# A share of the weight subtractions from VectorE to GpSimd, and all groups of modulation sums on VectorE, in a two-layer gMLP, attention and mixture-of-experts kernel

## The chip, the cores and the metric

The kernel runs on one core of one Trainium2 chip. The metric is the device time of one execution in microseconds; a run gives the median of several executions. The profile comes from one execution with the hardware profiler on, and its times are counted from the start of its span.

The engines of a core are TensorE (PE in the rows; PEld is its loading of weights), VectorE (DVE), ScalarE (ACT), GpSimd (POOL) and SyncE (SP), whose queue issues nearly all loads here. SBUF is the memory of the core that all engines read, PSUM the one in which TensorE leaves its results.

## What is computed

Two layers over 256 tokens of width 1024 (batch 1). Each layer modulates its input by shifts, scales and gates, which come from a conditioning vector `c` of 1024 through large matrices; the first layer mixes tokens with a gMLP, the second with an attention, and both end in a mixture of 64 experts with 8 of them chosen for each token, beside one shared expert.

```
def ada(c, w, b, n):
    m = jax.nn.silu(c) @ w + b
    return [t[:, None, :] for t in jnp.split(m, n, axis=-1)]

def gmlp_mixer(h, w_in, b_in, ln_g, ln_b, w_s, b_s, w_out):
    z = jax.nn.gelu(h @ w_in + b_in)
    u, v = jnp.split(z, 2, axis=-1)
    v = layernorm(v, ln_g, ln_b)
    ...
    sv = jnp.einsum('gts,bcsgd->bctgd', w, v) + b_s.T[None, None, :, :, None]
    return (u * sv.reshape(B, S, A_WIDTH)) @ w_out

def reference(x, c, ...):
    for i in range(DEPTH):                       # 2
        sh1, sc1, g1, sh2, sc2, g2 = ada(c, ada_w[i], ada_b[i], 6)
        h = modulate(rmsnorm(x, norm_mix[i]), sh1, sc1)
        if i < N_A_LAYERS:                       # layer 0
            y = gmlp_mixer(h, ...)
        else:                                    # layer 1
            if kv is None:
                kv = shared_kv(x, c, kv_norm, kv_ada_w, kv_ada_b, kv_w_k, kv_w_v)
            y = moba_mixer(h, ...)
        x = x + g1 * y
        h = modulate(rmsnorm(x, norm_ffn[i]), sh2, sc2)
        x = x + g2 * moe(h, ...)
    return rmsnorm(x, final_norm)
```

## The kernel before

The program is one core's, and its instructions stand on each engine in the order in which they are written (or recorded) below; an engine doesn't pass over one that waits. The stages are the gMLP phase of layer 0, its residual and the routing to experts, the loop over experts, the attention phase of layer 1, residual and routing again, and the second loop over experts.

**Steps and pieces.** The gMLP phase is a list of 48 steps: 16 of the token side (`Tok`, k = 0 to 15), 16 of the feature side (`Feat`, 16 to 31) and 16 of the output (`Out`, 32 to 47). Steps 6 to 47 run in the loop `for k in range(k, n + 16)`. A step multiplies with a 128x1024 part of a weight matrix. For accuracy the part is split in two: ScalarE copies it into the rounded type (`high`, an ACT `scr<-w`), and VectorE subtracts that copy from the original (`low`, a DVE `scr<-w,scr`); TensorE then needs both for three products (`mm3`). `split(steps, k, pool)` issues, in step k, the copy for step k + 3 and the subtraction for step k + 2. Four `scr` tiles are in turn. The attention phase (32 steps) does the same.

**Epilogues.** A `Tok` step ends in an addition on VectorE (`b<-acc`), an `Out` step in VectorE's `h<-wk` and the products after it; `b`, `s`, `h` are tiles of SBUF, `wk` and `acc` are results in PSUM. `BATCH_NORM_STATS2` gathers the layer norm's statistics from `b`.

**Groups of sums.** `ada` is done in groups of four loads of 1 MB: `("a", 2)` to `("a", 5)` for layer 0 (items 8 to 23), `("k", 0)` and `("k", 1)` for the keys and values (items 0 to 7), `("A", 0)` to `("A", 5)` for layer 1. A group listed in `VECTOR` is summed by VectorE: with each load come two instructions of 128x1024 that multiply a part of the load by one element of `silu(c)` and add it (`weigh`; the group's first one is a plain multiplication, `w<-w,cs`). The others are summed by TensorE in `strips`, sixteen matmuls in four takes, and closed by a matmul with `half`. `BEGIN` says in which step a load's sums may be begun, and `tick` lets out of each engine's list as many as the budget of the step (`BUDGET`) allows. In the kernel before, a5, k1 and A5 are summed by TensorE; k1's four takes stand in the routing of layer 0, behind the products `slot` of the routing.

**Loads.** All weights come through 14 slots of 1 MB, in the order of `QUEUE` on SP: one of `ITEMS` alternates with one of `MAIN` (the gMLP's matrices), and the three loads of the shared expert (`("s", 0)`, `wsh`) stand ahead of the last four of `wkva`. Behind them come the loads of experts whose number is known beforehand, and then those that wait for `order`, the list that the routing writes.

**The end of the phase.** `settle` and `close` let out what is left of the sums, `residual` adds the gated result to `xt`; then VectorE and TensorE work out in turns which expert takes which tokens, up to the cast to `order`. TensorE goes on with the gathering of tokens and the shared expert.

Of the kernel before, what the change touches and what calls it, by code (L numbers as in the profile page):

```python
# [33 lines left out]
PRE = 3  # L34
# [4 lines left out]
MAIN = [("i", i) for i in range(PRE, 16)] + [("o", i) for i in range(8)]  # L39
QUEUE = MAIN[:1] + [x for p in zip(ITEMS, MAIN[1:]) for x in p]  # L40
QUEUE += [("s", 0)] + ITEMS[len(MAIN) - 1:]

BEGIN = [(2 * PRE + 2 * i, x) for i, x in enumerate(ITEMS) if 2 * PRE + 2 * i < 46]
BUDGET = ((1.25, 0.9, 0.9), (1.25, 0.9, 0.9), (1.0, 0.9, 0.9))

# [11 lines left out]

VECTOR = [("a", 2), ("a", 3), ("k", 0), ("a", 4)] + [("A", i) for i in range(5)]

# [126 lines left out]
def tile_model(ctx: ExitStack, tc: tile.TileContext, A: dict, out: bass.AP):  # L186
# [86 lines left out]
    def low(t, src, eng=None):  # L273
        (eng or V).tensor_tensor(t[:, 1], src, t[:, 0], ALU.subtract)
# [267 lines left out]

    def split(steps, k, pool):

        if k + LA < len(steps):
            f = steps[k + LA]
            f.h = high(f.part(), pool)
        if 0 <= k + LA - 1 < len(steps):
            f = steps[k + LA - 1]
            low(f.h, f.part())  # L550

# [22 lines left out]
    def tick(tv, ts, tp):  # L574


        for f in list(active):
            if f.done():
                f.age = getattr(f, "age", 0) + 1
                if f.age > 1:  # L580
                    f.finish()
                    active.remove(f)
        for e, t in ((S, ts), (V, tv), (T, tp)):
            credit[e] = min(credit[e], 0) + t
            for f in active:
                while credit[e] > 0 and f.ops[e] and not (e is S and f.left(T)):
                    t, op = f.ops[e].pop(0)
                    op()
                    credit[e] -= t
# [610 lines left out]
    with phase("pb") as pool:  # L1200
# [170 lines left out]
        steps = []  # L1371
# [60 lines left out]
        for k in range(k, n + 16):  # L1432
# [3 lines left out]
            if k in (6, 10):  # L1436
                fetch_bv(512 * (k + 2) // 4, 512)
            split(steps, k, pool)
            e = k + 4 - n
# [20 lines left out]
            if k >= 42:  # L1460
                next(weighing, None)
            tick(*((0, 0.9, 0.9) if k > 45 else BUDGET[k // 16]))
        settle()
# [21 lines left out]
    with phase("pe") as pool:  # L1485
# [158 lines left out]
        for k in range(n):  # L1644
# [4 lines left out]
            if 0 <= j - 1 < 8:  # L1649
                pairs[j - 1].maxima()  # L1650
            split(steps, k, pool)
            if k:
# [18 lines left out]
            for c in range(2 * k - 24, 2 * k - 22) if 12 <= k < 16 else ():  # L1671
# [3 lines left out]
                G.tensor_tensor(hq[1][:, c, :], t, hq[0][:, c, :], ALU.subtract)  # L1675
            tick(*BUDGET1[k // 4])
            if k == WEIGH1 - 1:
# [93 lines left out]
```

## Time and profile before

| | us |
|---|---|
| median of three runs (lowest, highest) | 1399.44 (1397.13, 1403.96) |
| the profiled execution | 1401.17 |
| its span | 1399.4 |
| gMLP phase of layer 0 | 0 to 202 |
| residual, routing up to `order` | 202 to 221 |
| routing's rest, shared expert | 221 to 245 |
| loop over experts, layer 0 (from its start-up on) | 245 to 720 |
| attention phase of layer 1 | 720 to 872 |
| residual and routing, layer 1 | 872 to 960 |
| loop over experts, layer 1 | 960 to 1374 |

The stages are cut from the trace's timeline at instructions that can be named, such as the last matmul of a phase. Over the span PE is busy for 1339.6 us, DVE for 758.0, ACT for 452.2 and POOL for 57.6. The rows that follow are of three kinds: a window row gives the busy time of each engine in a stretch, with the granted clock of TensorE as a share of full speed; a group row puts like instructions of one engine together, with their count, their sum and the mean of one; a timeline row is one instruction (or some like ones in line) with its start and its duration, and in brackets the time that its engine stood idle before it.

### The profile page before, as it was taken

The page shows a single profiled execution, that of the slowest core. Times are in us where ns is not written, and L with a number is a line of the kernel's source. Part 1 is how long each engine was busy: PE and PEld are TensorE (multiplying, and loading weights), DVE is VectorE, ACT ScalarE, POOL GpSimd, SP SyncE. Part 2 cuts the span into 40 slices and gives each one's busy share as a digit, 9 for nine tenths or more (in the row PEclk, how much of TensorE's full clock was granted, in tenths as well). Part 3 has the DMA queues.
Part 4 walks back from the last instruction along what each step waited for, and adds up shares of the span by engine and source line. Part 5 has one row for each costly group of instructions (what it writes and reads, how often), then busy time and mean ns, then how long its engine had stood idle before and what let it go on. Part 6 is the DMA issues. An engine that isn't in the chain of part 4 may idle for free. (4 is left out here: it accounts for less than half of the span.)

```text
span 1399.4 us, 26932 instructions
## 1 busy us (share of the span) xinstructions
PE 1339.6 (96%) x10954; PEld 886.3 (63%) x10954; DVE 758.0 (54%) x1408; ACT 452.2 (32%) x921; POOL 57.6 (4%) x70
## 2 busy tenths in 40 slices
PE   8999999899999999998989999999999999999997
PEld 6899776555655555564649886765565556555553
DVE  3599945444455444444458866554444444444444
ACT  4444424122232222222344543322223222232222
POOL 1000002000000000000010320200000000000000
PEclk8899999999999999999999989999999999999999
DMA  9999876699999999999998855669999999999995
GB/s 387 332 342 360 313 267 240 262 402 425 426 426 425 426 373 426 426 426 426 426 408 318 295 205 216 271 230 394 418 426 426 426 426 425 426 426 426 426 426 218
DMA packets 91128, 516.60 MB, mean 369 GB/s; under 512 B 8308, under 2 KB 8436, under 8 KB 34934
## 3 DMA queue, kind: packets, MB, share of 16 engines
q1 hardware_dynamic: 90420, 513.77, 90.5%
q8 instruction: 88, 1.44, 0.4%
q10 hardware_dynamic: 580, 1.06, 0.2%
q14 instruction: 40, 0.33, 0.1%
HBM read 513.75 MB, written 1.05 MB: 368 GB/s over the span
## 5 line engine op out<-in xcount | busy, mean ns | idle before, releaser
L200 PE MATMUL wk<-w,b 128*32 128x256 f32 (+1 forms) x4928 | 415.6, 387 | 20.2 <-DMA w<-in_wexp_dram 20.2
L200 PEld LDWEIGHTS wk<-w,b 128*32 128x32 f32 (+1 forms) x4928 | 236.0, 123 | 166.2 <-DMA w<-in_wexp_dram 22.4
L200 DVE TENSOR_TENSOR s<-s,s 64x512 fp32r<-64x512 f32 x220 | 151.1, 687 | 123.5 <-ACT s L200 121.8
L200 PE MATMUL wk<-w,ht 128*32 128x512 f32 (+1 forms) x1232 | 211.5, 599 | 0.0
L200 ACT ACTIVATE b<-wk,adaT,sc 128x256 f32<-128x256 f32 x112 | 63.3, 565 | 285.6 <-DVE b L200 285.6
L200 DVE TENSOR_SCALAR b<-wk,sc,adaT 128x256 f32<-128x256 f32 x112 | 60.9, 544 | 156.0 <-PE wk L200 155.8
L200 PE MATMUL wk<-s,b 128*128 128x256 f32 (+2 forms) x1024 | 140.8, 287 | 0.0
L200 ACT CAST s<-s 64x512 fp32r<-64x512 f32 x220 | 134.3, 611 | 15.5 <-DVE s L200 12.8
L200 PEld LDWEIGHTS wk<-s,b 128*128 128x128 f32 (+1 forms) x1024 | 130.9, 187 | 10.3 <-issue 1.1
L200 PE MATMUL acc<-s,h 128*128 128x512 f32 x440 | 132.7, 423 | 0.4 <-DVEq L1147 0.4
L200 DVE TENSOR_TENSOR s<-wk,g 128x512 f32<-128x512 f32 x110 | 76.1, 692 | 89.2 <-PE wk L200 88.9
L200 PEld LDWEIGHTS wk<-w,ht 128*32 128x32 f32 (+1 forms) x1232 | 53.3, 121 | 99.7 <-issue 91.6
L200 ACT ACTIVATE h<-wk 64x256 f32<-64x256 f32 (+1 forms) x114 | 42.9, 376 | 211.7 <-PE wk L200 211.6
L200 DVE SCALAR_TENSOR_TENSOR h<-wk,ws,h 64x256 f32<-64x256 f32 x110 | 54.0, 491 | 98.1 <-ACT h L200 97.3
L200 DVE TENSOR_TENSOR scr<-w,scr 128x1024 fp32r<-128x1024 f32 x80 | 97.5, 1232 | 10.2 <-ACT scr L200 10.1
L200 ACT CAST scr<-w 128x1024 fp32r<-128x1024 f32 x80 | 83.1, 1047 | 51.7 <-PE wk L200 33.2
L200 PEld LDWEIGHTS acc<-s,h 128*128 128x128 f32 x440 | 74.4, 189 | 24.0 <-DVEq L1147 1.1
L200 ACT COPY ht<-wk 128x128 f32<-128x128 f32 x110 | 29.3, 266 | 185.4 <-PE wk L200 185.4
L200 PEld LDWEIGHTS wk<-ident,h 64*128 64x128 f32 (+1 forms) x226 | 22.5, 137 | 94.8 <-DVE h L200 93.9
L200 PE MATMUL wk<-hh,scr 128*128 128x256 f32 x576 | 73.0, 286 | 1.3 <-POOL hh L200 1.3
L200 PEld LDWEIGHTS wk<-hh,scr 128*128 128x128 f32 x576 | 70.5, 194 | 1.7 <-POOL hh L200 1.7
L200 PE MATMUL acc<-scr,hh 128*128 128x256 f32 x384 | 52.9, 299 | 4.8 <-DVE hh L200 4.5
(245 smaller groups left out, 1238.8 us busy)
## 6 DMA issues: line engine op xcount, KB each, us to landing
w<-in_wexp_dram SPq DMA_DIRECT2D x384, 1024.0 KB, 16.6
w<-in_wada_dram SPq DMA_DIRECT2D x48, 1024.0 KB, 7.6
w<-in_win_dram SPq DMA_DIRECT2D x16, 1024.0 KB, 7.5
w<-in_wqkvo_dram SPq DMA_DIRECT2D x16, 1024.0 KB, 7.8
w<-in_wkva_dram SPq DMA_DIRECT2D x8, 1024.0 KB, 6.8
w<-in_wout_dram SPq DMA_DIRECT2D x8, 1024.0 KB, 7.5
w<-in_wsh_dram SPq DMA_DIRECT2D x6, 1024.0 KB, 6.6
xt<-in_x_dram SPq DMA_DIRECT2D x1, 1024.0 KB, 6.4
```

Source lines behind the costliest of these rows:

```text
L200: r = f(*a, **k)
```

## The change

`split` takes an engine: in the odd steps that `HELP` lists, the subtraction goes to GpSimd instead of VectorE, twenty in the gMLP phase's loop (steps 7 to 47, the piece of step 9 on) and six in the attention phase (steps 1 to 11). `VECTOR` now has all groups, so a5, k1 and A5 join VectorE's sums and their strips are gone. The loads of `ITEMS` come at a pace of 1.75 steps instead of 2 and all ahead of the shared expert's. The budgets of VectorE's sums are lower, with 1.1 (0.6 in the attention phase) more in the steps in which GpSimd helps, and the last steps keep a budget. k1 is begun in the gMLP phase.

```
--- before.py
+++ after.py
@@ -37,11 +37,17 @@
 ITEMS = [("a", i) for i in range(8, 16)] + [("k", i) for i in range(4)]
 ITEMS += [("a", i) for i in range(16, 24)] + [("k", i) for i in range(4, 8)]
 MAIN = [("i", i) for i in range(PRE, 16)] + [("o", i) for i in range(8)]
-QUEUE = MAIN[:1] + [x for p in zip(ITEMS, MAIN[1:]) for x in p]
-QUEUE += [("s", 0)] + ITEMS[len(MAIN) - 1:]
-
-BEGIN = [(2 * PRE + 2 * i, x) for i, x in enumerate(ITEMS) if 2 * PRE + 2 * i < 46]
-BUDGET = ((1.25, 0.9, 0.9), (1.25, 0.9, 0.9), (1.0, 0.9, 0.9))
+
+PACE = 1.75
+QUEUE = sorted([(2 * i, x) for i, x in enumerate(MAIN)] + [(1 + PACE * i, x) for i, x in enumerate(ITEMS)],
+               key=lambda x: x[0])
+QUEUE = [x for _, x in QUEUE] + [("s", 0)]
+
+BEGIN = [(2 * PRE + int(PACE * i), x) for i, x in enumerate(ITEMS)]
+BUDGET = ((1.0, 0.9, 0.9), (1.0, 0.9, 0.9), (0.9, 0.9, 0.9))
+
+MORE = 1.1
+HELP = (range(7, 48, 2), range(1, 12, 2))
 
 
 AMONG = [(2, 0)]
@@ -55,7 +61,7 @@
 QUEUE1 = [x for _, x in QUEUE1] + [("s", 0)]
 BUDGET1 = ((1.8, 0.9, 0.9),) * 8
 
-VECTOR = [("a", 2), ("a", 3), ("k", 0), ("a", 4)] + [("A", i) for i in range(5)]
+VECTOR = [("a", i) for i in range(2, 6)] + [("k", i) for i in range(2)] + [("A", i) for i in range(6)]
 
 
 
@@ -540,14 +546,14 @@
                 for tt in range(2):
                     self.ep_(tt, self.p[tt])
 
-    def split(steps, k, pool):
+    def split(steps, k, pool, eng=None):
 
         if k + LA < len(steps):
             f = steps[k + LA]
             f.h = high(f.part(), pool)
         if 0 <= k + LA - 1 < len(steps):
             f = steps[k + LA - 1]
-            low(f.h, f.part())
+            low(f.h, f.part(), eng)
 
     sums = {}
     active = []
@@ -1435,7 +1441,7 @@
                     begin(x)
             if k in (6, 10):
                 fetch_bv(512 * (k + 2) // 4, 512)
-            split(steps, k, pool)
+            split(steps, k, pool, G if k in HELP[0] else V)
             e = k + 4 - n
             if k == n:
                 acc = accs()
@@ -1459,7 +1465,8 @@
                 flush(lambda f: f.dstT is adaT[0] and f.dst is None)
             if k >= 42:
                 next(weighing, None)
-            tick(*((0, 0.9, 0.9) if k > 45 else BUDGET[k // 16]))
+            tv, ts, tp = BUDGET[k // 16]
+            tick(tv + (MORE if k in HELP[0] else 0), ts, tp)
         settle()
         close()
         residual(xt, acc, g1[0])
@@ -1648,7 +1655,7 @@
             j = k - 17
             if 0 <= j - 1 < 8:
                 pairs[j - 1].maxima()
-            split(steps, k, pool)
+            split(steps, k, pool, G if k in HELP[1] else V)
             if k:
                 steps[k - 1].ep()
             if 0 <= j - 1 < 8:
@@ -1673,7 +1680,8 @@
                 S.activation(t, xT[c], AF.Identity, bias=adaT[1][:, c:c + 1], scale=scm[:, c:c + 1])
                 V.tensor_copy(hq[0][:, c, :], t)
                 G.tensor_tensor(hq[1][:, c, :], t, hq[0][:, c, :], ALU.subtract)
-            tick(*BUDGET1[k // 4])
+            tv, ts, tp = BUDGET1[k // 4]
+            tick(tv + (0.6 if k in HELP[1] else 0), ts, tp)
             if k == WEIGH1 - 1:
                 flush(lambda f: f.dst is None)
             if k >= WEIGH1:
```

Three places show how the instructions of the engines stand. The first is VectorE and GpSimd in the middle of the `Tok` steps. VectorE before:

```order
L200 TENSOR_TENSOR scr_848<-w_267,scr_848 128x1024
L200 TENSOR_TENSOR b_91_349<-acc_816,s_131_683 128x256
L200 TENSOR_TENSOR b_92_350<-acc_817,s_131_683 128x256
L200 SCALAR_TENSOR_TENSOR w_265<-w_265,cs,w_261 128x4x256
L200 SCALAR_TENSOR_TENSOR w_265<-w_265,cs 128x4x256
L200 TENSOR_TENSOR scr_875<-w_267,scr_875 128x1024
L200 BN_STATS bn_351<-b_91_349 128x6
L200 BN_STATS bn_352<-b_92_350 128x6
L200 TENSOR_TENSOR scr_910<-w_271,scr_910 128x1024
```

VectorE now:

```order
L206 SCALAR_TENSOR_TENSOR w_265<-w_265,cs,w_261 128x4x256
L206 SCALAR_TENSOR_TENSOR w_265<-w_265,cs 128x4x256
L206 TENSOR_TENSOR scr_848<-w_267,scr_848 128x1024
L206 TENSOR_TENSOR b_91_349<-acc_818,s_131_683 128x256
L206 TENSOR_TENSOR b_92_350<-acc_819,s_131_683 128x256
L206 BN_STATS bn_351<-b_91_349 128x6
L206 BN_STATS bn_352<-b_92_350 128x6
L206 TENSOR_TENSOR adaT_104<-wk_939,pk 128x8
L206 TENSOR_SCALAR w_269<-w_269,cs 128x4x256
L206 SCALAR_TENSOR_TENSOR w_269<-w_269,cs 128x4x256
L206 TENSOR_TENSOR scr_910<-w_273,scr_910 128x1024
```

GpSimd now, where before the `t_27` step was followed by the two of the routing (`t_162`, `t_165`):

```order
L206 TENSOR_TENSOR t_27_176<-t_23_163,mhalf 128x2
L206 TENSOR_TENSOR scr_685<-w_250,scr_685 128x1024
L206 TENSOR_TENSOR scr_749<-w_259,scr_749 128x1024
L206 TENSOR_TENSOR scr_815<-w_263,scr_815 128x1024
L206 TENSOR_TENSOR scr_877<-w_267,scr_877 128x1024
L206 TENSOR_TENSOR scr_951<-w_273,scr_951 128x1024
L206 TENSOR_TENSOR scr_1013<-w_277,scr_1013 128x1024
```

Of two subtractions that stood around the sums, one is now in GpSimd's queue, `scr_877` for example; the sums of VectorE stand one load further on beside the same epilogues.

The second is VectorE at the end of the gMLP phase, ahead of the residual, which begins with `s<-acc,g`. Before:

```order
L200 TENSOR_TENSOR s_256_1854<-b_90_348,s_256_1854 128x256
L200 TENSOR_TENSOR s_43_255<-s_43_255,sc_0_1857 128x512
L200 TENSOR_TENSOR scr_1876<-w_331,scr_1876 128x1024
L200 TENSOR_TENSOR s_263_1897<-b_90_348,s_263_1897 128x256
L200 TENSOR_TENSOR scr_1905<-w_331,scr_1905 128x1024
L200 TENSOR_TENSOR g_102_401<-wk_1963,g_102_401 128x512
L200 TENSOR_TENSOR g_102_401<-wk_1966,g_102_401 128x512
L200 TENSOR_TENSOR s_269_1969<-acc_1570,g_17_143 128x512
```

Now:

```order
L206 TENSOR_TENSOR s_43_255<-s_43_255,sc_0_1864 128x512
L206 SCALAR_TENSOR_TENSOR w_331<-w_331,cs 128x4x256
L206 TENSOR_TENSOR scr_1880<-w_337,scr_1880 128x1024
L206 TENSOR_TENSOR s_264_1901<-b_90_348,s_264_1901 128x256
L206 SCALAR_TENSOR_TENSOR w_335<-w_335,cs,w_331 128x4x256
L206 SCALAR_TENSOR_TENSOR w_335<-w_335,cs 128x4x256
L206 SCALAR_TENSOR_TENSOR w_339<-w_339,cs,w_335 128x4x256
L206 SCALAR_TENSOR_TENSOR w_339<-w_339,cs 128x4x256
L206 TENSOR_TENSOR kvT<-wk_1967,pk 128x8
L206 TENSOR_TENSOR s_269_1977<-acc_1574,g_17_143 128x512
```

The last subtraction of this end is GpSimd's; the last four weighted sums, k1's, and the addition that closes k1 (`kvT`) stand directly ahead of the residual, where the additions to the gate `g` stood.

The third is TensorE in the routing, from the products with `slot` on. Before:

```order
L200 LDWEIGHTS slot_2167
L200 MATMUL wk_2184<-identb,slot_2167 64x128
L200 MATMUL wk_2187<-w_339,cs 32x512 x4
L200 MATMUL wk_2187<-w_341,cs 32x512 x4
L200 MATMUL wk_2187<-w_343,cs 32x512 x4
L200 MATMUL wk_2187<-w_345,cs 32x512 x4
L200 MATMUL wk_2115<-b_299_2080,w_335 128x256 x4
L200 MATMUL wk_2115<-b_299_2080,w_333 128x256 x4
L200 MATMUL wk_2115<-b_299_2080,w_335 128x256 x4
```

Now:

```order
L206 LDWEIGHTS slot_2175
L206 MATMUL wk_2192<-identb,slot_2175 64x128
L206 MATMUL wk_2123<-b_299_2088,w_343 128x256 x4
L206 MATMUL wk_2123<-b_299_2088,w_341 128x256 x4
L206 MATMUL wk_2123<-b_299_2088,w_343 128x256 x4
L206 LDWEIGHTS slotT_2207
L206 MATMUL wk_2225<-pub_2211,slotT_2207 128x112
```

The four takes of `strips` between `slot` and the shared expert's `b,w` are gone, and the shared expert's parts lie in other slots, as its loads are issued later.

## Rows read from the trace of the kernel before

**Rows 1.** Windows: busy us and instructions by engine, granted clock, DMA share, GB/s.

```profile
core 0: us, PE busy (x) PEld busy (x) DVE busy (x) ACT busy (x) POOL busy (x), PEclk, DMA share, GB/s
62.00:138.00 76.00, 76.00 (x663) 75.81 (x661) 73.42 (x88) 39.48 (x59) 1.88 (x2) 1.00 0.94 343
138.00:191.00 53.00, 53.00 (x290) 40.47 (x290) 44.34 (x69) 19.02 (x30) 0.00 (x0) 1.00 0.86 309
191.00:202.00 11.00, 11.00 (x48) 8.07 (x45) 0.93 (x2) 0.59 (x1) 0.00 (x0) 1.00 0.28 92
202.00:221.00 19.00, 14.93 (x102) 11.79 (x100) 14.57 (x58) 11.21 (x25) 4.71 (x4) 0.99 0.78 322
221.00:245.00 24.00, 23.55 (x140) 17.38 (x139) 11.84 (x23) 7.44 (x14) 5.63 (x4) 0.94 0.67 235
...
290.00:720.00 430.00, 418.85 (x3697) 243.74 (x3691) 201.85 (x380) 118.57 (x254) 0.00 (x0) 0.99 1.00 421
...
736.00:771.00 35.00, 35.00 (x283) 34.79 (x283) 30.56 (x30) 13.97 (x20) 0.12 (x1) 0.95 0.87 330
```

**Rows 2.** Groups of DVE from 62.1 to 202.3: count, busy us, mean ns.

```profile
L200 DVE TENSOR_TENSOR scr<-w,scr 128x1024 fp32r<-128x1024 f32 x41 | 49.4, 1218 | 1.0 <-ACT scr L200 1.0
L200 DVE SCALAR_TENSOR_TENSOR w<-w,cs 128x1024 f32<-128x1024 f32 x16 | 20.6, 1284 | 0.5
...
L200 DVE SCALAR_TENSOR_TENSOR h<-wk,pk,b 128x256 f32<-128x256 f32 x16 | 7.7, 479 | 1.6 <-PE wk L200 1.6
...
L200 DVE BATCH_NORM_STATS2 bn<-b 128x6 f32<-128x512 f32 x8 | 5.1, 684 | 0.2 <-ACT b L200 0.2
L200 DVE TENSOR_TENSOR b<-acc,s 128x256 f32<-128x256 f32 x12 | 4.5, 417 | 0.0
...
L200 DVE TENSOR_SCALAR w<-w,cs 128x1024 f32<-128x1024 f32 x4 | 3.0, 745 | 0.0
```

**Rows 3.** Timeline of POOL and DVE at three places: start, us, engine, operation.

```profile
212.79 2.36 POOL L200 TENSOR_TENSOR b<-b,h 128x1024 f32<-128x1024 f32 x1 [2.50 <-ACT h L200]
...
224.26 2.37 POOL L200 TENSOR_TENSOR w<-w,g 128x1024 f32<-128x1024 f32 x1
...
786.68 2.40 POOL L200 TENSOR_TENSOR hh<-h,hh 128x256 fp32r<-128x256 f32 x2 [2.50 <-DVE hh L200]
...
212.75 1.22 DVE L200 TENSOR_TENSOR b<-b,wk 128x1024 f32<-128x1024 f32 x1 [0.62 <-ACT h L200]
...
224.32 2.39 DVE L200 SCALAR_TENSOR_TENSOR sm<-sm,sm 128x64 f32<-128x64 f32 x1
...
786.72 1.77 DVE L200 TENSOR_TENSOR scr<-w,scr 128x1024 fp32r<-128x1024 f32 x1
```

**Rows 4.** Group of PE from 62.1 to 202.3: the strips of a5.

```profile
L200 PE MATMUL wk<-w,cs 128*32 128x512 f32 x32 | 4.3, 604 | 0.0
```

**Rows 5.** Timeline of routing (PE, DVE, SP), and the page's row of loads.

```profile
215.57 1.89 PE L200 MATMUL wk<-b,w 128*128 128x256 f32 x8
...
221.21 4.93 PE L200 MATMUL wk<-w,cs 128*32 128x512 f32 x32
...
231.65 1.05 PE L200 MATMUL wk<-half,w 128*128 128x2 f32 x8
...
220.97 0.21 DVE L200 CAST order<-wk 1x64 int32<-1x64 f32 x1 [0.30 <-PE wk L200]
...
165.58 5.46 SPq L259 DMA_DIRECT2D w<-in_wsh_dram  x3
...
w<-in_wsh_dram SPq DMA_DIRECT2D x6, 1024.0 KB, 6.6
```

**Rows 6.** Timeline of DVE in the attention phase, with its idle time in brackets.

```profile
770.48 0.17 DVE L200 TENSOR_TENSOR adaT<-wk,pk 128x8 f32<-128x8 f32 x1 [3.77 <-PE wk L200]
...
862.21 0.42 DVE L200 TENSOR_TENSOR b<-wk,b 128x256 fp32r<-128x256 f32 x1 [2.29 <-ACT b L200]
...
870.53 0.69 DVE L200 TENSOR_TENSOR g<-wk,g 128x512 f32<-128x512 f32 x1 [3.11 <-PE wk L200]
```

**Rows 7.** Window from 50 to 60 us, in the columns of Rows 1.

```profile
50.00:60.00 10.00, 8.53 (x64) 7.63 (x65) 4.73 (x11) 5.08 (x8) 0.00 (x0) 0.83 0.95 334
```

More of the change, by code (lines that the diff above doesn't have):

```diff
@@ L39 @@
 MAIN = [("i", i) for i in range(PRE, 16)] + [("o", i) for i in range(8)]
[L40 to L44, printed above, removed]
+PACE = 1.75
+QUEUE = sorted([(2 * i, x) for i, x in enumerate(MAIN)] + [(1 + PACE * i, x) for i, x in enumerate(ITEMS)],
+               key=lambda x: x[0])
+QUEUE = [x for _, x in QUEUE] + [("s", 0)]
+BEGIN = [(2 * PRE + int(PACE * i), x) for i, x in enumerate(ITEMS)]
+BUDGET = ((1.0, 0.9, 0.9), (1.0, 0.9, 0.9), (0.9, 0.9, 0.9))
+MORE = 1.1
+HELP = (range(7, 48, 2), range(1, 12, 2))
 AMONG = [(2, 0)]
@@ L56 @@
 BUDGET1 = ((1.8, 0.9, 0.9),) * 8
-VECTOR = [("a", 2), ("a", 3), ("k", 0), ("a", 4)] + [("A", i) for i in range(5)]
+VECTOR = [("a", i) for i in range(2, 6)] + [("k", i) for i in range(2)] + [("A", i) for i in range(6)]
 SH = -1
@@ L541, in ep, with split @@
                     self.ep_(tt, self.p[tt])
-    def split(steps, k, pool):
+    def split(steps, k, pool, eng=None):
         if k + LA < len(steps):
@@ L549, in split @@
             f = steps[k + LA - 1]
-            low(f.h, f.part())
+            low(f.h, f.part(), eng)
     sums = {}
@@ L1437, in tile_model @@
                 fetch_bv(512 * (k + 2) // 4, 512)
-            split(steps, k, pool)
+            split(steps, k, pool, G if k in HELP[0] else V)
             e = k + 4 - n
@@ L1461, in tile_model @@
                 next(weighing, None)
-            tick(*((0, 0.9, 0.9) if k > 45 else BUDGET[k // 16]))
+            tv, ts, tp = BUDGET[k // 16]
+            tick(tv + (MORE if k in HELP[0] else 0), ts, tp)
         settle()
@@ L1650, in tile_model @@
                 pairs[j - 1].maxima()
-            split(steps, k, pool)
+            split(steps, k, pool, G if k in HELP[1] else V)
             if k:
@@ L1675, in tile_model @@
                 G.tensor_tensor(hq[1][:, c, :], t, hq[0][:, c, :], ALU.subtract)
-            tick(*BUDGET1[k // 4])
+            tv, ts, tp = BUDGET1[k // 4]
+            tick(tv + (0.6 if k in HELP[1] else 0), ts, tp)
             if k == WEIGH1 - 1:
```

## The prediction

> **What bounds the kernel now.** I read the page first, for the shares of the engines, and then cut the span into stages, because a share over the whole span mixes stages with different limits. Over the whole span TensorE looks like the one bound; the stages say otherwise [rows 1]. The gMLP loop (62 to 202 us) keeps TensorE busy in every microsecond: 76.00 of 76, 53.00 of 53, 11.00 of 11. Beside it VectorE has 73.42 of 76, then 44.34 of 53, then almost nothing (0.93 of 11). So two engines are at their limit up to 138 us, and VectorE has about 20 us to spare afterwards. At 221 the order of the experts is known and TensorE works on through routing and shared expert, 23.55 of 24 us. From 290 the expert loop moves 421 GB/s with a DMA share of 1.00: it is bound by loads, with a fixed number of bytes, so a stage ahead of it passes its delay on to the end one for one. GpSimd has nearly no work: 1.88 us in the gMLP loop up to 138 and none from there to its end.
>
> **GpSimd's subtractions in the gMLP loop.** Twenty of the 41 subtractions leave VectorE, at 1218 ns each [rows 2]: 24.4 us less. What comes instead for a5 and k1, groups of four loads each, is 14 weighted sums of 1284 ns and 2 first ones of 745: 19.5 us more. VectorE then has 118.7 - 24.4 + 19.5 = 113.8 us, five less than before, and the edit looks good. The price of the same subtraction on GpSimd is the question. A GpSimd subtraction of two 128x1024 tiles takes 2.36 us [rows 3], so twenty are 47.2 us.
>
> Whether these 47.2 us lie beside VectorE's work or in line with it decides the case, and three pairs of rows speak on it [rows 3]. At 224.26 GpSimd multiplies for 2.37 us; VectorE's 128x64 step begins at 224.32 and ends only with it, after 2.39 us, though 128x64 is a sixteenth of the columns of a subtraction that takes 1.22. Both engines read two tiles of SBUF there, and one stood still for the whole of the other's instruction. At 212.75 and 212.79 the two run together, VectorE 1.22 us and GpSimd 2.36, neither longer than alone; there one of VectorE's two inputs is a TensorE result in PSUM (b<-b,wk). I read it so: instructions with two SBUF inputs shut each other out, those with one don't. At 786.72 a subtraction on VectorE takes 1.77 us instead of 1.22, behind one of GpSimd's that had begun 0.04 us earlier. The moved subtraction stays a two-input one, and on VectorE the remaining subtractions and the weighted sums are of the kind that must wait.
>
> The Trainium skill ("SBUF — State Buffer", Who interferes with whom) says that a VectorE instruction with two SBUF inputs contends with a GpSimd one that reads SBUF, and one with at most one such input, outside the faster modes, does not; the rows at 224 and 212 agree. By it the sum of this part would be the next paragraph's, so nothing in that sum hangs on it.
>
> Without overlap the two engines share 113.8 + 47.2 = 161.0 us. VectorE operations with one input in PSUM, or one input at all, are the epilogues h<-wk (7.7), b<-acc (4.5) and the statistics (5.1), 17.3 us together [rows 2]; if all of them fell under GpSimd's work, 143.7 us. Between these ends lies the answer: nothing steers the epilogues to the moments when GpSimd runs, they wait for TensorE, and they are 15% of VectorE's time. I take 2 us of overlap, near the no-overlap end: 159 us. The loop had 140 us (62 to 202) with TensorE full, and the last weighted sums now stand in VectorE's queue directly ahead of the residual, so VectorE's end is the loop's: **+19** (bounds +4 and +21; +24 if VectorE also keeps the 2.6 us of waits of its first 76). TensorE meanwhile loses a5's strips, 4.3 us [rows 4], and gains the small totals of k1, so its own need is some 137.5: it is late only because it waits for the pieces. The steps wait on both engines in turn, so each late GpSimd piece holds up TensorE and, through the epilogues, VectorE's queue too.
>
> **Routing.** k1's strips (4.93 us at 221.21) and its closing matmuls (1.05 at 231.65) go away [rows 5]. They stand on a TensorE that is full between 221 and 245, in front of the shared expert and the gathering of tokens, and nothing else fills the place: **-6** for the start of the expert loop, bounds -2 (the loads, not TensorE, open the loop) and -6.
>
> **Loads.** On SP's queue the shared expert's three loads now stand behind all of wkva; the last two of wout stand behind two and three of wkva as well. They were issued at 165.58 and landed after 6.6 us, and their first use is at 215.57 [rows 5]: some 40 us of cover, against four loads passed, 4.2 MB, or 14 us at the 309 GB/s of that stretch [rows 1]. If that cover were gone, each microsecond would fall on the shared expert, TensorE's full stretch. Three ScalarE copies that closed the strips go; ScalarE has 39.48 busy of 76, so I count nothing. Cost 0, bounds 0 and +3.
>
> **The attention phase.** Six subtractions move to GpSimd, 6 x 2.36 against 6 x 1.22, +6.8 us on the shared reading, in a stretch in which VectorE has 30.56 of 35 us [rows 1] and then waits 3.77 us for TensorE [rows 6]: of 6.8, the 4.4 idle hides most, and +2 to +3 are left. A5's eight sums, 0.75 + 7 x 1.28 = 9.7 us, come to VectorE at the end of the phase, where it idles 2.29 at 862.21 and 3.11 at 870.53 [rows 6], 5.4 in all: about +4, against A5's strips on TensorE, four takes of 1.06 as in the 4.3 above: -4.3. Net **+1**, bounds -4 and +6.
>
> **The sum.** +19 - 6 + 0 + 1 = +14. The profiled run took 1401.2 us, its span of 1399.4 and 1.8 around it; with 14 it is 1415.2. The median before, 1399.4, lies 1.7 below that run, so the predicted median is 1413.
>
> **Rivals.** *A, faster: the two engines share little.* For it: VectorE loses 5 us of work, and both kinds of pairing stand in the trace only a few times each. Against it: the row at 224.32. It decides if a GpSimd subtraction costs VectorE under 1.2 us of its 2.36: TensorE's need of 137.5 us less VectorE's 113.8 leaves 23.7 for twenty. Then TensorE sets the loop (137.5 instead of 140: -2.5), routing gives -6, the attention phase -3: 1388. The Trainium skill ("Perfetto Trace Analysis", Optimizing Scalar/DVE Operations) allows this way, saying that with VectorE saturated "offloading some work to Scalar (or even GPSIMD) may make sense", and adds that between those two it "might not help"; A needs the first half, and the row at 224 is on the side of the second.
>
> *B, no change: all one-input work overlaps.* The same exclusion, but the epilogues fall under GpSimd's time: 143.7 us, +4, with -6 and +1: 1399. It needs a queue order that I don't see written anywhere.
>
> *C, slower still: TensorE's clock.* With 19 us of waits in 159, TensorE is busy 8.8 tenths; in the stretch from 50 to 60 us it was busy 8.53 and the granted clock was 0.83 of full speed, a mean of the levels 1.2 and 2.4 GHz [rows 7]. If it went so through the whole loop, 137.5 us of work would take 166 instead of 140: +26, and with -6 and +1 1420, or a few more. Against it: from 202 to 221 us TensorE was busy only 14.93 of 19 us and had 0.99 [rows 1], so waits of this share need not lower it.
>
> That the change doesn't do what it says I leave out: in the instruction order the 26 subtractions stand on GpSimd and the strips of the three groups are gone.
>
> **How the numbers follow.** Forecast (1408 to 1419, from the bounds on overlap) 0.60; A 0.14; B 0.16; C 0.10. The prediction is 1413. For 8 in 10 I take in B and C and leave A out: 1397 to 1425. About 0.5%, 7 us, is what a measurement of this kernel can tell from no change; A is below it, B within, forecast and C above: faster 0.14, same 0.16, slower 0.70.
>
> **What would show it.** In the profile after: GpSimd busy some 61 us more (26 x 2.36) or longer, if its own instructions are lengthened by waits. VectorE's subtractions and weighted sums with means well above 1.22 and 1.28 us (their waits lie inside the instruction). TensorE with idle time ahead of the matmuls on the pieces, released by GpSimd or VectorE. The order of the experts at about 240 instead of 220.97 [rows 5], and the loop saturated some 13 us later. It would be wrong in the size if VectorE's means stay at 1.22 and 1.28 beside 47 us of GpSimd work (A), or if only the one-input operations run under GpSimd (B); a granted clock under 0.9 between 62 and 220 is C. If the expert loop doesn't start later by what the gMLP loop lost, the step on loads passing the delay on has failed.

## The result, and the profile after

The changed kernel takes 1412.12 us in the median of five runs (1410.58 to 1422.34), against 1399.44 before (1397.13 to 1404.56, five runs): 12.7 us more, a ratio of 1.010 with a 95% interval of 1.0072 to 1.0128. It is slower by more than the 0.5% that can be told from no change. Ratios leave out runs more than 1.5% above the fastest of their kernel, which are two of the eleven of sums_only below. Its profiled execution took 1410.7 us, with a span of 1408.9; the one before took 1401.2. So the two profiles lie 9.5 us apart, three less than the medians do, because the profiled run before was above its median and the one after below.

Four points in both traces tell where the time goes. The cast to `order` moves from 220.97 to 237.34 us, 16.4 later. The gathering of tokens, TensorE's 32 matmuls `wk<-s,b`, ends 10.5 later (245.11 and 255.61). The second `order`, of layer 1, is 10.0 later (896.94 and 906.92), and the end 9.5 later. The loss is made in the gMLP phase, a third of it is given back in the routing, and the rest stays to the end.

The windows of the kernel after, in the columns of [rows 1]; the third covers the gMLP loop, from the first matmul of step 6 to the addition that closes k1 (`kvT`):

```profile
62.00:138.00 76.00, 67.82 (x564) 66.88 (x563) 72.10 (x64) 31.67 (x47) 35.12 (x14) 0.98 0.87 312
138.00:191.00 53.00, 48.11 (x276) 40.66 (x276) 52.42 (x60) 18.02 (x29) 18.86 (x7) 1.00 0.82 285
60.20:218.70 158.50, 142.51 (x974) 128.79 (x973) 151.44 (x155) 56.97 (x88) 59.74 (x22) 0.98 0.77 275
```

Against [rows 1] TensorE no longer fills the loop, 67.82 of 76 us and 48.11 of 53, while VectorE stands at 72.10 and 52.42. GpSimd has gone from 1.88 us to 35.12 and from nothing to 18.86. VectorE is the engine that is nearly always busy: 151.44 of the loop's 158.5 us.

The groups of VectorE from 62.1 to 222 us and GpSimd's group of subtractions from 60 to 220 us (count, busy us, mean ns), which answer to [rows 2]; the last two lines are of the kernel before:

```profile
L206 DVE SCALAR_TENSOR_TENSOR w<-w,cs 128x1024 f32<-128x1024 f32 x24 | 41.2, 1716 | 0.6
L206 DVE SCALAR_TENSOR_TENSOR w<-w,cs,w 128x1024 f32<-128x1024 f32 x18 | 30.9, 1717 | 0.1
L206 DVE TENSOR_TENSOR scr<-w,scr 128x1024 fp32r<-128x1024 f32 x21 | 29.9, 1426 | 0.0
L206 DVE TENSOR_TENSOR b<-b,h 128x256 f32<-128x256 f32 x16 | 11.9, 746 | 0.6
L206 DVE TENSOR_SCALAR w<-w,cs 128x1024 f32<-128x1024 f32 x6 | 9.2, 1536 | 0.0
L206 DVE SCALAR_TENSOR_TENSOR h<-wk,pk,b 128x256 f32<-128x256 f32 x16 | 7.6, 474 | 0.0
L206 DVE TENSOR_SCALAR b<-b,t,t 128x1024 f32<-128x1024 f32 x4 | 7.4, 1860 | 0.0
...
L206 DVE TENSOR_TENSOR b<-acc,s 128x256 f32<-128x256 f32 x12 | 4.5, 414 | 0.0
...
L206 POOL TENSOR_TENSOR scr<-w,scr 128x1024 fp32r<-128x1024 f32 x20 | 57.9, 2896 | 132.9 <-ACT scr L206 132.9
...
L200 DVE TENSOR_TENSOR b<-b,h 128x256 f32<-128x256 f32 x16 | 6.8, 426 | 0.6
...
L200 DVE TENSOR_SCALAR b<-b,t,t 128x1024 f32<-128x1024 f32 x4 | 3.2, 808 | 0.0
```

These are the rows to learn to read. A weighted sum took 1284 ns before and takes 1716, a subtraction 1218 and now 1426, a product `b<-b,h` 426 and now 746. Nothing in these instructions changed; a wait for the other engine lies inside the instruction and is booked as busy time. The epilogues with an input in PSUM stand as they were: `h<-wk` 479 and 474, `b<-acc` 417 and 414. GpSimd's own subtractions take 2896 ns, where an undisturbed one took 2.36 us [rows 3].

Single instructions of GpSimd, VectorE and TensorE in the kernel after (start, us, and in brackets the idle time before):

```profile
107.77 6.56 POOL L206 TENSOR_TENSOR scr<-w,scr 128x1024 fp32r<-128x1024 f32 x2
...
130.10 2.74 POOL L206 TENSOR_TENSOR scr<-w,scr 128x1024 fp32r<-128x1024 f32 x1 [4.46 <-ACT scr L206]
...
111.97 2.91 DVE L206 TENSOR_SCALAR b<-b,t,t 128x1024 f32<-128x1024 f32 x1
...
129.35 1.22 DVE L206 TENSOR_TENSOR scr<-w,scr 128x1024 fp32r<-128x1024 f32 x1
130.48 3.44 DVE L206 SCALAR_TENSOR_TENSOR w<-w,cs,w 128x1024 f32<-128x1024 f32 x1
...
111.02 2.86 PE L206 MATMUL wk<-hh,scr 128*128 128x256 f32 x22 [1.58 <-POOL scr L206]
...
123.41 5.71 PE L206 MATMUL wk<-hh,scr 128*128 128x256 f32 x48 [1.85 <-DVE scr L206]
```

GpSimd begins a subtraction at 130.10 and ends it at 132.84. VectorE's weighted sum begins at 130.48 and ends 3.44 us later, at 133.92: 2.36 us of it lie before GpSimd's end and 1.08 behind it, where it takes 1.28 alone (rows of VectorE overlap a little at their ends). At 111.97 a scaling of the layer norm, with one input in SBUF, takes 2.91 us instead of the 0.81 that it has in the trace before; it waited as well. And TensorE stands still for 1.58 us for a GpSimd piece and for 1.85 us for one of VectorE's. The first is the only wait of the loop that TensorE's matmuls have for GpSimd; those put down to VectorE come to 13.4 us. So what reaches TensorE is mostly VectorE's lateness, not that of GpSimd's pieces.

The end of the loop, the routing and the shared expert's loads, and as the last line the gathering of tokens in the kernel before:

```profile
218.70 0.17 DVE L206 TENSOR_TENSOR kvT<-wk,pk 128x8 f32<-128x8 f32 x1 [2.14 <-PE wk L206]
...
237.34 0.21 DVE L206 CAST order<-wk 1x64 int32<-1x64 f32 x1 [0.28 <-PE wk L206]
...
231.99 1.89 PE L206 MATMUL wk<-b,w 128*128 128x256 f32 x8
...
237.47 5.45 PE L206 MATMUL wk<-b,w 128*128 128x256 f32 x24
...
251.44 4.17 PE L206 MATMUL wk<-s,b 128*128 128x256 f32 x32
...
188.51 5.90 SPq L265 DMA_DIRECT2D w<-in_wsh_dram  x3
...
240.93 4.18 PE L200 MATMUL wk<-s,b 128*128 128x256 f32 x32
```

VectorE's last weighted sums end at 216.5 and TensorE's last product at 217.0; then the closing of k1 (`kvT`) and the residual. The strips of k1 are gone from behind `slot`: `wk<-b,w` stands at 237.47, right after the cast, where [rows 5] had 4.93 us of strips first.

### The profile page after: what moved, and what is told of

It is laid out like the page before. It is cut to its first block, busy times and chain, and to the rows that moved or that the text cites. A ratio compares the mean times of both kernels' runs of the same rounds, so it can differ in the third digit from the quotient of the medians.

```text
span 1408.9 us, 26803 instructions
## 1 busy us (share of the span) xinstructions
PE 1328.1 (94%) x10866; PEld 886.2 (63%) x10866; DVE 799.9 (57%) x1406; ACT 448.6 (32%) x918; POOL 132.5 (9%) x96
## 5 line engine op out<-in xcount | busy, mean ns | idle before, releaser
L206 POOL TENSOR_TENSOR t<-t,mhalf 128x2 f32<-128x2 f32 (+1 forms) x7 | 5.4, 773 | 1028.9 <-DVE t L206 1028.9
L206 POOL TENSOR_TENSOR scr<-w,scr 128x1024 fp32r<-128x1024 f32 x26 | 75.0, 2887 | 155.5 <-ACT scr L206 155.5
L206 DVE TENSOR_TENSOR scr<-w,scr 128x1024 fp32r<-128x1024 f32 x54 | 73.3, 1363 | 13.3 <-ACT scr L206 13.2
## 6 DMA issues: line engine op xcount, KB each, us to landing
w<-in_wexp_dram SPq DMA_DIRECT2D x384, 1024.0 KB, 16.4
```

What stands on the lines that cost most here:

```text
L206: r = f(*a, **k)
```

## Experiments

Two theories were set against each other. **E**: GpSimd and VectorE shut each other out where both read two tiles of SBUF, so GpSimd's subtractions cost nearly their whole time. **L**: the sums added on VectorE are what fills it, and GpSimd's help is a gain. Later a third came in, on TensorE's clock.

The table shows all kernels. "Loop" goes from the first matmul of step 6 to the cast to `order`; "start" from there until 100 MB have been moved in all, added up from the trace's transfers, which lies in the saturated part of the first expert loop; "attention" from 275 MB to the second `order`. They are of the profiled run, and each holds the falls of TensorE's clock that this one execution had: that of sums_only, for example, took 1383.1 us at a mean clock of 0.986, 18 us less than its median. The ratio is that of the runs to the runs of the kernel before on the same chip, with its interval; "clock" is the median over the runs of the mean granted clock, with that of the kernel before beside it where it was taken with the same runs. The last column is an estimate: within one kernel the runs with a lower mean clock are the longer ones, 1.2 us for each 0.001 over all 191 runs whose clock is on record (correlation -0.93); brought to 0.977 by that line, the mean of a kernel's runs is set against that of the kernel before on the same chip. For the changed kernel, whose comparison runs have no clock on record, the kernel before on the four chips of the other runs stands in (1400.9 to 1402.4).

| kernel | loop | start | attention | median us | ratio | clock (before) | us against before at a like clock (estimate) |
|---|---|---|---|---|---|---|---|
| before | 158.6 | 90.4 | 169.5 | 1399.4 | | | |
| after | 177.1 | 84.1 | 168.8 | 1412.1 | 1.0100 (1.0072 to 1.0128) | 0.977 | +11 to +12.5 |
| sums_only | 160.3 | 84.1 | 161.2 | 1401.0 | 0.9985 (0.9958 to 1.0011) | 0.972 (0.977) | -7.2 |
| help_only | 170.2 | 89.2 | 163.5 | 1414.4 | 1.0109 (1.0066 to 1.0152) | 0.972 (0.977) | +7.4 |
| dummy_two | 186.1 | 85.8 | 170.2 | 1428.6 | 1.0198 (1.0156 to 1.0240) | 0.967 (0.977) | +14.7 |
| dummy_none | 161.7 | 88.8 | 170.3 | 1403.0 | 1.0002 (0.9971 to 1.0033) | 0.970 (0.977) | -7.8 |
| help_late | 167.2 | 84.1 | 170.5 | 1402.5 | 1.0014 (0.9981 to 1.0048) | 0.976 (0.977) | -1.4 |
| help_attn | 158.7 | 90.6 | 175.9 | 1403.7 | 1.0008 (0.9983 to 1.0032) | 0.977 (0.977) | +2.4 |
| sums_gmlp | 160.2 | 87.4 | 169.8 | 1402.1 | 1.0004 (0.9982 to 1.0025) | 0.972 (0.977) | -5.4 |
| k1_only | 162.6 | 85.3 | 172.8 | 1401.5 | 1.0003 (0.9976 to 1.0030) | 0.977 (0.977) | -1.4 |
| wide_sums | 160.2 | 83.9 | 165.8 | 1392.2 | 0.9951 (0.9923 to 0.9979) | 0.979 (0.979) | -7.9 |
| wide_before | 160.3 | 89.9 | 170.0 | 1401.3 | 1.0005 (0.9982 to 1.0027) | 0.977 (0.979) | -1.2 |
| wide_after | 176.8 | 82.5 | 173.6 | 1418.5 | 1.0141 (1.0095 to 1.0187) | 0.972 (0.977) | +11.4 |

**sums_only: the change without GpSimd.**

```
-            split(steps, k, pool, G if k in HELP[0] else V)
+            split(steps, k, pool)
...
-            split(steps, k, pool, G if k in HELP[1] else V)
+            split(steps, k, pool)
```

> The changed kernel with all 26 moved subtractions back on VectorE; its sums, loads and budgets stay. Theory E (GpSimd and VectorE shut each other out where both have two SBUF inputs): VectorE then has 113.8 + 24.4 = 138.2 us of work in a gMLP loop of which TensorE needs 137.5, so the loop takes 140 to 144 instead of 158, routing keeps its gain of 6 and the attention phase its small gain: 1393 to 1400 us, 12 to 19 below the changed kernel. Rival L (the added sums fill VectorE, GpSimd's help lies beside it and is a gain): VectorE gets 24 us more than in the changed kernel, so slower than that, over 1415. Rival C (waits lower TensorE's clock): between the two, with a granted clock under 0.9 in the changed kernel's loop and 1.00 here.

The loop is 160.3 us instead of 177.1, and the median 11 us below the changed kernel's: L is out. The weighted sums have their old duration, as VectorE's groups from 60 to 205 us show:

```profile
L206 DVE TENSOR_TENSOR scr<-w,scr 128x1024 fp32r<-128x1024 f32 x41 | 49.7, 1219 | 0.0
L206 DVE SCALAR_TENSOR_TENSOR w<-w,cs 128x1024 f32<-128x1024 f32 x24 | 30.8, 1283 | 0.5
```

But the kernel is at 1401, not at the 1393 to 1400 that E gave: as before, where the loop's +1.7 and the start's -6.3 promise a gain. Its runs have a clock of 0.972 against 0.977; at a like clock it is some 7 us faster than the kernel before. That gap is taken up further below.

**help_only: GpSimd's subtractions alone, in the kernel before.**

```
-            low(f.h, f.part())
+            low(f.h, f.part(), eng)
...
-            split(steps, k, pool)
+            split(steps, k, pool, G if 7 <= k and k % 2 else V)
```

> The kernel before with one edit: the twenty subtractions of the gMLP loop on GpSimd; no sum is moved. Theory E: 118.7 - 24.4 + 47.2 = 141.5 us for the two engines together without overlap, about 10 less with what the changed kernel showed; but up to 138 us VectorE had no slack before, so the early part is late and TensorE, full all along, can't make it up: 1404 to 1411 us. Rival L: VectorE loses 24 us, nothing is late: 1396 to 1400.

The loop is 11.6 us longer and the ratio 1.0109. VectorE was given 24 us less to do and the kernel became slower, with no sum moved at all. VectorE's groups, and GpSimd's:

```profile
L200 DVE TENSOR_TENSOR scr<-w,scr 128x1024 fp32r<-128x1024 f32 x21 | 33.3, 1589 | 0.0
L200 DVE SCALAR_TENSOR_TENSOR w<-w,cs 128x1024 f32<-128x1024 f32 x16 | 31.0, 1936 | 0.5
...
L200 POOL TENSOR_TENSOR scr<-w,scr 128x1024 fp32r<-128x1024 f32 x20 | 56.5, 2826 | 129.6 <-ACT scr L200 129.6
```

The weighted sums take 1936 ns here. The median, 1414.4, is above the 1404 to 1411 expected; at a like clock it would be about 1409, so that excess is the granted clock's, 0.972 against 0.977.

**dummy_two and dummy_none: GpSimd work that nobody waits for.** Both are sums_only with this added in the odd steps, the first with the subtraction, the second with fills that read nothing (a copy of one column ahead of them keeps the step). Nothing reads `junkt`.

```
+            if k in HELP[0] and k + 2 < len(steps):
+                f0 = steps[k + 2].h[:, 0].rearrange("p a b -> p (a b)")
+                for hf in range(2):
+                    G.tensor_tensor(junkt, f0[:, 512 * hf:512 * hf + 512], f0[:, 512 * hf:512 * hf + 512], ALU.subtract)
```

```
+                G.tensor_copy(junkt[:, 0:1], f0[:, 0:1])
+                for _ in range(4):
+                    G.memset(junkt, 0.0)
```

> The kernel sums_only with work added that nobody reads: in each odd step of the gMLP loop GpSimd subtracts the halves of the step's rounded piece from themselves, two instructions of 128x512 with two SBUF inputs, some 2.5 us together, twenty times. No result of GpSimd is waited for by TensorE. Theory E: about 50 us of GpSimd work against a VectorE with 138 of 140 us, some 10 to 15 of it under one-input work: the loop grows by 25 to 40, so 1418 to 1438 us. Rival P (what costs is that a piece comes later from the slower GpSimd, 2.4 to 2.9 us instead of 1.2): nothing waits for these instructions, so as sums_only within 3 us.

> As dummy_two, but GpSimd only fills a tile with zeros, four instructions of 128x512 a step and a copy of 128x1 ahead of them that keeps the step: about as long (2 to 2.5 us a step, by the 0.2 us of a 128x128 fill) and with no SBUF input. Theory E: the fills read nothing, so VectorE isn't held: as sums_only within 4 us. Rival: any busy GpSimd holds VectorE: as dummy_two.

VectorE's groups from 60 to 205 us and GpSimd's from 60 to 220, of dummy_two:

```profile
L206 DVE TENSOR_TENSOR scr<-w,scr 128x1024 fp32r<-128x1024 f32 x37 | 52.5, 1425 | 0.0
L206 DVE SCALAR_TENSOR_TENSOR w<-w,cs 128x1024 f32<-128x1024 f32 x21 | 33.9, 1615 | 0.5
...
L206 POOL TENSOR_TENSOR junkt<-scr 128x512 f32<-128x512 f32 x40 | 66.4, 1661 | 132.4 <-ACT scr L206 130.6
```

and of dummy_none:

```profile
L206 DVE TENSOR_TENSOR scr<-w,scr 128x1024 fp32r<-128x1024 f32 x41 | 49.7, 1218 | 0.0
L206 DVE SCALAR_TENSOR_TENSOR w<-w,cs 128x1024 f32<-128x1024 f32 x24 | 30.8, 1282 | 0.5
...
L206 POOL MEMSET junkt<- 128x512 f32 x80 | 45.3, 566 | 4.6
L206 POOL COPY junkt<-scr 128x1 f32<-128x1 f32 x20 | 15.0, 752 | 111.0 <-ACT scr L206 110.9
```

This pair decides. GpSimd is busy in both, 66.4 us with the subtractions and 60.3 with fills and copies. Beside the fills VectorE's instructions have their undisturbed 1218 and 1282 ns and the loop grows by 1.4 us; beside the subtractions they take 1425 and 1615, and it grows by 25.8. No result of GpSimd is used, so a later piece isn't needed for the cost (rival P); what the fills lack and the subtractions have is GpSimd's reading while VectorE wants to read. The medians show it too: 1428.6 against 1403.0.

**help_late: only the last eight pieces on GpSimd.**

```
-            split(steps, k, pool)
+            split(steps, k, pool, G if k in HELP[0] and k > 30 else V)
```

> sums_only with the subtractions of the last eight odd pieces of the gMLP loop (steps 33 to 47, issued from step 31 on) on GpSimd. Theory E (each GpSimd piece costs the pair its whole time, less what falls under one-input work): twenty pieces made the loop 16.8 us longer (177.1 against 160.3), so eight give +5 to +8 by share, or less, down to +2, because TensorE, not VectorE, sets the pace of the last third in the kernel before: 1403 to 1409. Rival (the early pieces alone did it, since VectorE is full only up to 138 us): as sums_only, 1400 to 1402.

The loop takes 167.2, 6.9 us more than sums_only's 160.3, by eight pieces: 0.86 us for each, as the 16.8 us of all twenty give 0.84. The price goes by count, also in the last third. That isn't a test of pieces beside an idle VectorE: it had slack there in the kernel before, but in sums_only, which this run edits, it has none, 52.30 of 53 us:

```profile
138.00:191.00 53.00, 52.02 (x264) 41.75 (x264) 52.30 (x78) 20.24 (x33) 0.00 (x0) 1.00 0.81 300
```

In the kernel before, with that slack, help_only's twenty pieces cost 0.58 us of loop each. The medians (1402.5 and 1401.0) show less than the loop does and their intervals overlap, but the clocks differ, 0.976 and 0.972; at a like clock the two kernels lie 5.8 us apart.

**help_attn: the six pieces of the attention phase alone.** The edit is that of help_only, with `G if k in range(1, 12, 2) else V` in the attention phase.

> The kernel before with the six subtractions of the attention phase on GpSimd and nothing else. Theory E: +6.8 us of work on the shared pair against 4.4 us idle, so the attention phase gets +1 to +4, 1400 to 1405 us. Rival L (GpSimd's work lies beside): VectorE is 7.3 us shorter where it has 30.56 of 35 us, so 1396 to 1400.

The window from 736 to 771 us and two of VectorE's groups in it, beside the last row of [rows 1]:

```profile
736.00:771.00 35.00, 29.58 (x229) 28.77 (x229) 32.61 (x23) 13.20 (x20) 14.32 (x9) 0.95 0.75 272
...
L200 DVE TENSOR_TENSOR scr<-w,scr 128x1024 fp32r<-128x1024 f32 x5 | 10.4, 2087 | 0.0
...
L200 DVE SCALAR_TENSOR_TENSOR w<-w,cs 128x1024 f32<-128x1024 f32 x6 | 11.5, 1922 | 0.1
```

TensorE falls from 35.00 busy to 29.58. The attention phase is 6.4 us longer in the profiled run, the median 1.6 above the kernel before, with an interval that holds no change: a cost of a few us, some 2.4 at a like clock, not resolved better than that.

**sums_gmlp and k1_only: where did sums_only's gain go?** Both are sums_only with fewer groups on VectorE.

```
-VECTOR = [("a", i) for i in range(2, 6)] + [("k", i) for i in range(2)] + [("A", i) for i in range(6)]
+VECTOR = [("a", i) for i in range(2, 6)] + [("k", i) for i in range(2)] + [("A", i) for i in range(5)]
```

For k1_only `range(2, 6)` is `range(2, 5)` as well.

> sums_only with the layer 1 group A5 back on TensorE's strips, so that the attention phase stands as in the kernel before and only the gMLP loop (a5, k1 on VectorE, loads first) and the routing differ. Theory E: loop +1 to +2, routing -6, prelude as it was: 1393 to 1398 us. If sums_only's missing gain was eaten by A5's eight sums in the attention phase, this one is 4 to 6 us faster than sums_only; if it was eaten by TensorE's clock (mean granted clock about 0.972 in its runs against 0.977 before), it stays near 1399 to 1401 with that lower clock.

> As sums_gmlp, but a5 too stays on TensorE's strips: only k1 moves to VectorE and out of the routing. VectorE then has 128.5 us of work and TensorE 142: TensorE sets the loop, +1 to +3, routing -6: 1394 to 1398 us. It tells whether the fuller VectorE (138.2 of 140 in sums_gmlp) costs anything: if so, this one is the faster of the two by 2 to 4 us.

Neither is faster than the kernel before, so A5's sums did not eat the gain. sums_gmlp has the lower clock, 0.972 against 0.977. A mean lower by 0.005 is 1% of the span more at 1.2 instead of 2.4 GHz, 14 us, in which up to 7 us of TensorE's work are lost: as much as was missing. k1_only doesn't fit that: its clock is that of the kernel before, its loop is 4.0 us longer than before (TensorE then has a5's strips and k1's closing) and its start 5.1 shorter, which should leave a gain of about 1, and at a like clock it has 1.4; the expectation of 1394 to 1398 failed at the loop, +4.0 instead of +1 to +3, and at the start, -5.1 instead of -6. TensorE's timeline in sums_gmlp at two places, its windows there (columns of [rows 1]), and as the last two lines the same place in sums_only:

```profile
833.31 2.99 PE L206 MATMUL acc<-scr,b 128*128 128x512 f32 x12
...
840.12 2.90 PE L206 MATMUL wk<-onesf,w 128*128 128x1 f32 x16
842.88 5.20 PE L206 MATMUL acc<-scr,b 128*128 128x512 f32 x12
...
200.89 2.08 PE L206 MATMUL wk<-onesf,w 128*128 128x1 f32 x16 [0.92 <-PE acc L206]
202.83 3.38 PE L206 MATMUL wk<-onesf,ident 128*128 128x128 f32 x15
...
200.00:205.00 5.00, 4.11 (x26) 4.14 (x27) 2.78 (x6) 0.00 (x0) 0.00 (x0) 0.75 0.82 295
840.00:845.00 5.00, 5.00 (x25) 4.61 (x24) 1.95 (x5) 0.00 (x0) 0.01 (x1) 0.58 0.12 23
...
831.89 1.90 PE L206 MATMUL wk<-onesf,w 128*128 128x1 f32 x16
...
833.65 3.01 PE L206 MATMUL acc<-scr,b 128*128 128x512 f32 x12
```

At 840.12 stand the 16 matmuls of one column that close a group summed by VectorE, 2.90 us. After them a step of 12 matmuls takes 5.20 us, where the same step takes 2.99 at 833.31, and the granted clock of the window is 0.58: most of it at 1.2 GHz. The same at 200.89, ahead of the residual, with 0.75. Every group that moves to VectorE brings such a closing in place of its strips. But a closing of one column isn't always followed by a fall: in sums_only's trace the same one takes 1.90 us, the step behind it 3.01, and the clock stays at 1.00. Of the ten traces with closings of one column, the last one of the attention phase is followed by a fall in six; in those of before, after, sums_only and help_only it is not.

**wide_sums, wide_before and wide_after: closings of 64 columns.** The sum of the group stays the weight, and 64 columns of ones move instead of one; the first of 64 equal columns is read.

```
-                    T.matmul(pt[:, j:j + 1], w, onesf[:, 0:1], start=True, stop=True)
+                    T.matmul(pt[:, j], w, onesf[:, 0:64], start=True, stop=True)
```

> sums_only with one edit: the eight matmuls that close a group summed by VectorE (the sum is the weight, a column of ones moves) move 64 columns of ones instead of one; the first of the 64 equal columns is read. In the profiles of sums_gmlp and dummy_none TensorE's granted clock falls to 0.5 while or right after such a closing stands (16 matmuls of one column, at 201, 802 and 840 us). Theory N (these one-column stretches bring on the falls that eat the gain of sums_only): falls at these places go, the mean clock of the runs rises from 0.972 to 0.976 or more, 1393 to 1398 us. Rival W (the falls come from the waits for the softmax and the residual around those places): clock and time as sums_only, 1400 to 1403, plus 0 to 2 us for the columns.

> The kernel before with the same edit of the closings (its k1, a5 and A5 stay on strips and close otherwise). Theory N: it has the same closings at other places, most at a full TensorE, and its mean clock is 0.977 already: 1396 to 1402. Rival W: 1400 to 1404. Beside wide_sums it tells whether the change's sums, without GpSimd, are worth their 6 us once the clock is held.

TensorE in wide_sums at the same places, and its windows:

```profile
836.91 1.95 PE L206 MATMUL wk<-onesf,w 128*128 128x64 f32 x16
838.67 3.00 PE L206 MATMUL acc<-scr,b 128*128 128x512 f32 x12
...
201.18 1.97 PE L206 MATMUL wk<-onesf,w 128*128 128x64 f32 x16 [0.92 <-PE acc L206]
202.99 2.00 PE L206 MATMUL wk<-onesf,ident 128*128 128x128 f32 x16
...
200.00:205.00 5.00, 4.07 (x34) 3.65 (x32) 2.89 (x5) 0.00 (x0) 0.00 (x0) 1.00 0.74 261
800.00:805.00 5.00, 5.00 (x25) 5.00 (x25) 2.59 (x7) 0.39 (x3) 0.00 (x0) 0.50 0.35 116
840.00:845.00 5.00, 5.00 (x39) 4.14 (x38) 4.51 (x10) 3.00 (x11) 1.61 (x2) 1.00 0.90 300
```

The closings take 1.95 and 1.97 us, no longer than those of one column (2.08 at 200.89), the step behind takes 3.00, and the clock is 1.00 at both. A fall at about 800 us stays (0.50); it begins at 796.7, before the closing there (798.75), while TensorE waits for parts of the softmax. The median clock is 0.979, that of the kernel before on this chip, where sums_only had 0.972 on its own, and the time 1392.2: a ratio of 0.9951 (0.9923 to 0.9979). It is faster than the kernel before and than the changed one. The same edit does nothing for the kernel before (1.0005). So the sums of the change are worth some 7 us if GpSimd stays out of it and the clock holds: at a like clock sums_only has that gain already (-7.2 against -7.9), and what it lacked in the median is the clock. That the wider closings brought the clock back is not shown. The ratios of sums_only and wide_sums have overlapping intervals and come from two chips; behind the last closing of the attention phase the three traces with 64 columns have no fall, but four of the ten with one column have none either; and in wide_after the clock falls with a closing of 64 columns at 760.5 us.

> The changed kernel with the closings of 64 columns, so wide_sums with the 26 subtractions on GpSimd. Theory E: the difference from wide_sums is the price of GpSimd's subtractions with the clock held on both sides, 16.8 us in the gMLP loop and 1 to 3 in the attention phase: 1392 + 18 to 20 = 1410 to 1412. If the one-column closings had cost the changed kernel as much as sums_only, it is 5 to 8 us under the changed kernel's 1412, at 1404 to 1407, and GpSimd's price only 12 to 15.

It came out at 1418.5, ratio 1.0141, above the 1410 to 1412 expected. The loop is 176.8 us against wide_sums' 160.2, 16.6 more, as expected; the clock is 0.972 against 0.979, and at a like clock it is some 18 us behind wide_sums, as expected too. What lowers its clock isn't shown: the changed kernel has the same pieces on GpSimd and 0.977, and this is four runs. Whether it is really slower than the changed kernel can't be told: the two intervals overlap. The wider closings do nothing for the changed kernel that can be seen.

## Why the prediction was right

The prediction was 1413 in a range of 1397 to 1425, with 0.70 on slower; 1412.1 came out. Its steps:

**The gMLP loop, +19.** Measured from the first matmul of step 6 to `order` +18.5 (177.1 against 158.6); `order` itself is only 16.4 later because the stretch ahead of step 6 was 2.1 shorter in the profiled run after. The sum of 159 us is 158.5 in the window shown, but two of its terms were off and cancelled, so that the size is partly luck. VectorE's work is 113.8 by the forecast and it was busy for 151.4, so GpSimd's 47.2 us cost it 37.6 and 9.6 lay beside VectorE's work, not 2. (Taken from sums_only, where VectorE is busy for 136.5 us of its loop, 112.1 without the twenty subtractions, the overlap is 7.9.) Against that VectorE stood idle for 7.1 us, 3.8 of them ahead of the closings of k0 and k1, which I had put at the bound and not into the sum. The overlap was mis-sized by a factor of four to five, near the low end, where I had argued that nothing steers it. That argument itself gives more than 2: GpSimd is at work in 59.7 of 158.5 us, and that share of the 17.3 us of epilogues is 6.5. The sentence that each late GpSimd piece holds up TensorE did not hold either: TensorE's matmuls waited 1.6 us for GpSimd and 13.4 for VectorE.

**The exclusion itself.** Shown by dummy_two against dummy_none, and by the pair at 130 us. The reading of [rows 3] that one-input instructions don't wait was too wide: the scalings with one input in SBUF (`b<-b,t,t`, `w<-w,cs`) went from 808 to 1860 ns and from 745 to 1536. I had left them out of the overlap, so the sum didn't suffer. The Trainium skill ("SBUF — State Buffer", Who interferes with whom) has them: VectorE's faster modes, which a `tensor_scalar` can enter, contend with GpSimd even with a single input. The durations here agree.

**Routing, -6.** 24.1 us from `order` to the end of the gathering before (220.97 to 245.11), 18.3 after: -5.9, and -6.3 up to 100 MB. Up to 1.4 us of it may be the clock, 0.94 in that stretch before and 1.00 after. It came through to the second `order`, as the step on the bound expert loop said: help_only and help_attn, which keep k1's strips, have starts of 89.2 and 90.6. But sums_gmlp and dummy_none, which lack them, have 87.4 and 88.8, so one profiled run does not resolve the start to better than a few us.

**Loads, 0.** The shared expert's loads are issued at 188.51 and used at 231.99; TensorE does not wait for them.

**The attention phase, +1.** The terms of the forecast, 2.5 + 4 - 4.3, add up to +2.2, not +1. It was -0.7 in the profiled runs; GpSimd's six pieces alone +6.4 in one profiled run and +1.6 in the median. The bounds of -4 and +6 hold it in all but that one run.

**The sum, +14.** The profiled runs lie 9.5 us apart: 16.4 at `order`, 5.9 given back in the routing, 0.5 more up to the second `order` and 0.5 behind it. The medians lie 12.7 apart, and by the estimate at a like clock 11 to 12.5, so the direction and most of the size stand, and that 1413 came within 1 us of the median is luck in part.

**The rivals.** A (the engines share little) and L are out by sums_only and dummy_two. B, full overlap, needed 17.3 us of overlap; 8 to 10 were there. C was put at a clock of 0.83 through the loop, and that did not come: the window from 60.2 to 218.7 has 0.98. In a smaller size it isn't shown either: with GpSimd's pieces the runs' clock is lower in help_only (0.972), wide_after (0.972) and dummy_two (0.967), but not in the changed kernel (0.977), and it is lower without them in sums_only (0.972) and dummy_none (0.970).

**What stays open.** What lowers the clock of the kernels with more sums on VectorE, and whether the wider closings or chance gave wide_sums its clock. Of the changed kernel's 12.7 us hardly more than 1 or 2 are the clock's, by the estimate at a like clock.

## What to carry to other kernels

Moving two-input elementwise work from a full VectorE to GpSimd is not offloading: the pair works in turns, and at 2.36 us against 1.22 each moved instruction cost 0.84 us of loop time where VectorE was full throughout, and 0.58 in the kernel before, where it had slack from 138 us on. Before such a move, look in the trace for a GpSimd instruction beside a VectorE one and compare durations with the undisturbed ones; the wait is hidden in the mean of a group, not in idle time. When a gain of a few us on TensorE doesn't show in the median, compare the mean granted clock of the runs before looking for another culprit: 0.005 of it were 6 us here.

## What the runs showed that I had not expected

Runs of one kernel differ by up to 1.7% (sums_only, 1383.1 to 1406.4 us) with a mean clock from 0.986 to 0.967. In sums_gmlp, sixteen matmuls that move one column each were followed by half clock (0.58 and 0.75 in 5 us windows), and with 64 columns each, in 1.95 us, wide_sums stayed at 1.00 there; sums_only stayed at 1.00 with one column too, at 831.89, so the columns are not shown to be the cause. GpSimd's fills of 128x512 take 566 ns and cost VectorE nothing, 45 us of them in one loop.
